# Retention and latent-attention decoder in float32 on one core: x reloaded block by block, three seven-product row pairs in u_1, an ordered first load

## The chip, the cores and the metric

The kernel runs on one core of a Trainium2 chip. The metric is the device time of one execution in microseconds (us); lower is better. In the text PE is the matrix engine (PEld its weight loads), DVE the vector engine, ACT the scalar engine, POOL the GpSimd engine, and SP the engine whose queue issues most transfers. "Granted clock" is the share of PE's full clock that the chip allowed.

## The reference

x is 256 tokens by 2048 features in float32. A retention layer and its MLP are followed by one key and value projection that is shared, an MLA layer and its MLP:

```python
h = rms_norm(x, norm_mix[0])
x = x + retention(h, ret_w_in[0], ret_w_out[0], ret_cos, ret_sin)
x = x + sq_relu_mlp(rms_norm(x, norm_mlp[0]), mlp_w1[0], mlp_w2[0])
k_nope, k_pe, v = mla_shared_kv(rms_norm(x, kv_norm_in), ...)
h = rms_norm(x, norm_mix[1])
x = x + mla_attention(h, ..., k_nope, k_pe, v, mla_cos, mla_sin)
x = x + sq_relu_mlp(rms_norm(x, norm_mlp[1]), mlp_w1[1], mlp_w2[1])

def sq_relu_mlp(h, w1, w2):
    return jnp.square(jax.nn.relu(h @ w1)) @ w2
```

An MLP has 8192 hidden features, so w1 and w2 are 64 MB each, and the two MLPs hold most of the work.

## The kernel before, in words

**Products.** A float32 product is made of three matmuls on operands that are split into a high part and a low part: high x high, high x low, low x high. ACT makes the high part of a weight (CAST ..._wh), DVE subtracts it from the weight to get the low part (TENSOR_TENSOR ..._wl), and both must be there before PE can use them. Weights come in quads: 1 MB, 256 rows by 1024 columns, loaded by one transfer from SP's queue into one of four `raw` buffers. `quad` has two forms. With eight products (24 matmuls of 512 columns) it needs two casts on ACT and two lows on DVE. With seven (a Strassen scheme, 21 matmuls) DVE first adds parts of the weight (`u[0]`, `u[1]`, three instructions) and then there are four casts and four lows.

**Stages.** `gemm_pair` runs eight quads against one pair of sums in PSUM; this is a row pair. An MLP has four groups. Each group has two row pairs of w1 (u_0 and u_1 for the first group, then u_2, u_3 and so on, to u_7) and then two of w2 (d_00, d_01, then d_10 to d_31; the first digit is the group). A layer's number stands behind the letter: u0_7 is u_7 of the first MLP, and u0_73 is quad 3 of it. The views and the orders leave some of the numbers out.

**Hidden blocks.** When a u row pair ends, `pair_out` copies its sums out of PSUM, `summed` joins them, ACT applies relu with the norm's factor (ACTIVATE u_c<-u_c,n_r), copies the result as two 16-bit halves (COPY hid_h<-u_c), four transposing transfers on SP turn them (hid_t), ACT joins the halves (COPY hid_u<-hid_t), squares and casts them, and DVE makes the low part. hid_60 is the first piece of u_6, hid_61 the second; a piece holds two blocks. All this of u_6 runs while PE is in u_7, and that of u_7 while PE is in d_30.

**The residual.** x lies in HBM (`x_home`, tiles xh). d_00 to d_21 add their results there with accumulating transfers from POOL's queue (`to_home`). For the last pair of second products, and likewise for the retention output and the attention output, x must be in SBUF: `x_tiles` allocates four tiles and loads them with eight transfers of 256 KB on POOL's queue (L629, called at L1405 for the MLPs). `bring` is due every two quads.

**The order of the work.** Nothing is issued as it is written. All instructions are recorded in `Plan` with an estimated cost. `forward` is a list scheduler which, on each engine, takes the instruction with the earliest due date among those ready. `latest` runs backward over the result to give better due dates, and both run six rounds (`schedule`); the best is emitted. Each engine then runs its list in order, and waits wherever an operand is not there. All traced instructions therefore have the line L480, that of the emitter. `behind(op, other)` keeps an instruction from being issued ahead of another, and `low_part[0]` is the latest low recorded.

**The start.** `start`, `gemm_two` and `first_inputs` load the first retention weights (rq) and the transposed x (x0t). The first chunk's first half is cut in two, so that the first matmul can start early. DVE casts the positions to float (pos_f), and POOL makes the angles of the rotary tables from them (tab_ang, tab_k, tab_kh); DVE then takes a low part of the table (tab_kl).

Of the kernel before, what the change touches and what calls it, by code (L numbers as in the profile page):

```python
# [120 lines left out]
class Op:  # L121
    __slots__ = ("engine", "method", "args", "kw", "number", "before", "after", "cost", "took", "due", "start", "end",
                 "new", "left", "ready", "made", "held", "moves", "behind", "ahead")


class Plan:
# [19 lines left out]
    def record(self, engine, method, args, kw):  # L146
        op = Op()
        op.engine, op.method, op.args, op.kw = self.ENGINES[engine], (engine, method), args, kw
        op.number, op.before, op.after, op.new = len(self.ops), {}, [], []
        op.made = op.held = None  # L150
        op.behind, op.ahead = set(), []
# [104 lines left out]
    def latest(self):  # L256
# [3 lines left out]
        behind = {op: [] for op in self.ops}  # L260
        limit, free = {}, dict.fromkeys(self.LATENCY, 0.0)
        waiting = {e: [] for e in free}
# [50 lines left out]
    def forward(self):  # L313
# [73 lines left out]
        while True:  # L387
            best = None
            for e in free:
                w, r = waiting[e], ready[e]  # L390
                while w and w[0][0] <= free[e]:
                    _, _, op = heapq.heappop(w)
                    heapq.heappush(r, (op.due, op.number, op))
                at = free[e] if r else w[0][0] if w else None
# [10 lines left out]
            if not ready[e]:  # L405
                while waiting[e] and waiting[e][0][0] <= at:
                    _, _, op = heapq.heappop(waiting[e])
                    heapq.heappush(ready[e], (op.due, op.number, op))
            _, _, op = heapq.heappop(ready[e])
# [138 lines left out]
def yoco(ctx: ExitStack, tc: tile.TileContext, a):  # L548
# [195 lines left out]

    def stream(w, chunk, cols, name, use, done=None, before=None):

        raw = nc.tile(pool, [P, 2048], F32, f"{name}_raw", "raw", 4)
        if before is None:
            nc.sync.dma_start(raw[:, :cols], w[chunk])
        n = cols // 2  # L750
        for half in range(2):
            wh = nc.tile(pool, [P, 1024], F32R, f"{name}_wh{half}", "wh", 5)
            wl = nc.tile(pool, [P, 1024], F32R, f"{name}_wl{half}", "wl", 5)
            cuts = 1
            if before is not None:
                cuts = 1 if half or chunk else 2
                m = n // cuts
                for i in range(cuts):
                    lo = half * n + i * m
                    nc.sync.dma_start(raw[:, lo : lo + m], w[chunk][:, lo : lo + m])  # L760
                    if i == 0:
                        before(half)
            m = n // cuts
            for i in range(cuts):
                lo = half * n + i * m
                low_part[0] = split(wh[:, i * m : (i + 1) * m], wl[:, i * m : (i + 1) * m], raw[:, lo : lo + m])
            use(half, wh, wl)
# [19 lines left out]

    def four_t(acc, act, k0, nk, wh, wl):

        for j in range(4):  # L790
            k = k0 + j
# [24 lines left out]
    def gemm_two(w, act, nk, names, before, done):  # L816
# [3 lines left out]
        for g in range(n):  # L820
            stream(
                w, g, 2048, f"{names[0]}{g}", lambda half, wh, wl: four_t(acc[half], act, g * 4, nk, wh, wl),
                (lambda: done(acc)) if g == n - 1 else None, lambda half: before(g) if half == 0 else None,
            )

# [321 lines left out]
    def first_inputs(c):  # L1147

        t = f2k([2, S], f"x0t_{c}")
        if c:  # L1150
            nc.sync.dma_start(t, a["xt"][:, 2 * c : 2 * c + 2, :])
        else:
            for j in range(2):
                nc.sync.dma_start(t[:, j], a["xt"][:, j, :])
        v = act_tile(f"a0_{c}")
# [656 lines left out]
```

## Time and profile before

| what | value |
|---|---|
| median of 3 runs | 2428.97 us (2428.86 to 2429.07) |
| profiled execution, its own time | 2431.72 us |
| span of the profiled execution | 2429.9 us |
| mean granted clock | 0.996 |
| PE busy | 2405.2 us, 99% |
| DVE busy | 2262.6 us, 93% |
| ACT busy | 1852.3 us, 76% |
| POOL busy | 219.2 us, 9% |
| HBM traffic | 478.09 MB read, 39.85 MB written |

PE is busy nearly all the time, so idle time of another engine matters only where PE ends up waiting for it. "Busy" hides one thing: a matmul at a lower granted clock counts as busy for longer. A row of windows gives, for a stretch A:B, its length, the busy time of PE, PEld, DVE, ACT and POOL (with the number of instructions), the granted clock, the busy share of the DMA engines and GB/s. A row of waits reads: engine, tile, "<-" engine and tile waited for, us in total, times, longest. In a timeline a row holds start, duration, engine, line, operation, out<-in, shapes, and in brackets the idle time ahead of it and what ended that.

### The profile page before, as it was taken

Reading aid. Unit: us, or ns where it says so; the run is one execution under the profiler, and the core shown is the slowest. Engines: PE = TensorE matmul, PEld = TensorE weight load, DVE = VectorE, ACT = ScalarE, POOL = GpSimd, SP = SyncE. Lnnn points to the kernel's source line nnn. Section 1 sums busy time; section 2 is a strip of 40 time slices with the busy share of each in tenths; the row PEclk is TensorE's granted clock in tenths of the full one; section 3 lists DMA queues with packets and bytes.
Section 4 is the critical chain, followed back from the end, with each engine's and each line's share of the span. In section 5 each row is a group of like instructions: output and inputs, shape, how many; then the busy total and the mean of one; then the engine's idle time right before and its main releaser. Section 6 shows DMA issues by size and latency. Waiting matters only on the chain. (4 is left out here: it accounts for less than half of the span.)

```text
span 2429.9 us, 31583 instructions
## 1 busy us (share of the span) xinstructions
PE 2405.2 (99%) x11190; PEld 2013.8 (83%) x11190; DVE 2262.6 (93%) x3002; ACT 1852.3 (76%) x2613; POOL 219.2 (9%) x245
## 2 busy tenths in 40 slices
PE   9999999999999999999999999999999999999999
PEld 7888888888887788888877888998887888888877
DVE  8999999989999999999989998877899999999989
ACT  7666766667787969769769979677879688697795
POOL 3000001011000010010110001110000100100100
PEclk9999999999999999999999999999999999999999
DMA  8566669667585698799897766545767997987974
GB/s 339 191 203 210 204 210 256 201 200 237 200 260 189 220 271 228 242 262 231 239 269 223 217 226 190 169 145 188 220 208 215 257 238 233 258 240 243 265 235 145
DMA packets 197136, 545.18 MB, mean 224 GB/s; under 512 B 115441, under 2 KB 116977, under 8 KB 143729
## 3 DMA queue, kind: packets, MB, share of 16 engines
q1 hardware_dynamic: 174720, 495.84, 63.5%
q0 software_dynamic: 21248, 46.15, 9.9%
q8 instruction: 87, 1.43, 0.2%
q10 hardware_dynamic: 1008, 1.18, 0.2%
q14 instruction: 73, 0.59, 0.1%
HBM read 478.09 MB, written 39.85 MB: 213 GB/s over the span
## 5 line engine op out<-in xcount | busy, mean ns | idle before, releaser
L480 PE MATMUL d_c<-d_wh,hid 128*128 128x512 f32 x1412 | 455.1, 391 | 4.2 <-ACT hid L480 4.2
L480 PE MATMUL u_c<-u_wh,n 128*128 128x512 f32 x1328 | 428.9, 390 | 3.1 <-ACT u_wh L480 3.1
L480 PEld LDWEIGHTS d_c<-d_wh,hid 128*128 128x128 f32 x1412 | 266.5, 189 | 61.4 <-ACT hid L480 5.0
L480 PEld LDWEIGHTS u_c<-u_wh,n 128*128 128x128 f32 x1328 | 249.7, 188 | 55.3 <-ACT u_wh L480 3.8
L480 DVE TENSOR_TENSOR d_wl<-d_raw,d_wh 128x1024 fp32r<-128x1024 f32 (+1 forms) x256 | 279.2, 1108 | 5.4 <-ACT d_wh L480 5.4
L480 ACT CAST u_wh<-u_raw 128x1024 fp32r<-128x1024 f32 (+1 forms) x256 | 235.9, 952 | 62.5 <-PE u_c L480 49.1
L480 DVE TENSOR_TENSOR u_wl<-u_raw,u_wh 128x1024 fp32r<-128x1024 f32 (+1 forms) x256 | 272.6, 1095 | 8.9 <-ACT u_wh L480 8.6
L480 PE MATMUL d_c<-d_wl,hid 128*128 128x512 f32 x706 | 275.8, 391 | 0.1
L480 ACT CAST d_wh<-d_raw 128x1024 fp32r<-128x1024 f32 (+1 forms) x256 | 240.4, 964 | 40.7 <-PE d_c L480 23.2
L480 PE MATMUL u_c<-u_wl,n 128*128 128x512 f32 x664 | 259.4, 391 | 3.1 <-DVE u_wl L480 3.1
L480 PE MATMUL rp_c<-rp_wh,a 128*128 128x512 f32 x640 | 206.6, 390 | 0.0
L480 ACT CAST rp_wh<-rp_raw 128x1024 fp32r<-128x1024 f32 (+1 forms) x128 | 118.4, 944 | 65.6 <-PE rp_c L480 36.7
L480 DVE TENSOR_TENSOR u_wl<-u_u,u_wh 128x1024 fp32r<-128x1024 f32 x120 | 145.3, 1220 | 22.3 <-ACT u_wh L480 21.6
L480 ACT CAST d_wh<-d_u 128x1024 fp32r<-128x1024 f32 x106 | 108.8, 1052 | 69.4 <-DVE d_u L480 59.6
L480 ACT CAST u_wh<-u_u 128x1024 fp32r<-128x1024 f32 x120 | 125.4, 1052 | 43.2 <-PE u_c L480 19.4
L480 PEld LDWEIGHTS d_c<-d_wl,hid 128*128 128x128 f32 x706 | 133.2, 189 | 28.2 <-DVE d_wl L480 0.5
L480 PEld LDWEIGHTS u_c<-u_wl,n 128*128 128x128 f32 x664 | 124.7, 188 | 32.4 <-DVE u_wl L480 6.6
L480 DVE TENSOR_TENSOR rp_wl<-rp_raw,rp_wh 128x1024 fp32r<-128x1024 f32 (+1 forms) x128 | 136.1, 1092 | 8.6 <-ACT rp_wh L480 7.8
L480 PEld LDWEIGHTS rp_c<-rp_wh,a 128*128 128x128 f32 x640 | 120.1, 188 | 26.0 <-DVE rk_u L480 0.9
L480 DVE TENSOR_TENSOR d_wl<-d_u,d_wh 128x1024 fp32r<-128x1024 f32 x106 | 127.6, 1220 | 5.9 <-ACT d_wh L480 5.6
L480 PE MATMUL u_p<-u_wh,n_more 128*128 128x512 f32 x360 | 122.7, 395 | 2.2 <-ACT u_wh L480 2.2
L480 PE MATMUL rp_c<-rp_wl,a 128*128 128x512 f32 x320 | 124.5, 389 | 0.0
(464 smaller groups left out, 5941.4 us busy)
## 6 DMA issues: line engine op xcount, KB each, us to landing
u_raw<-in_mlp_w SPq DMA_DIRECT2D x128, 1024.0 KB, 6.3
d_raw<-in_mlp_w SPq DMA_DIRECT2D x128, 1024.0 KB, 5.3
rp_raw<-in_ret_w_gv SPq DMA_DIRECT2D x64, 1024.0 KB, 5.0
ro_raw<-in_ret_w_out SPq DMA_DIRECT2D x32, 1024.0 KB, 5.1
uq_raw<-in_mla_w_uq SPq DMA_DIRECT2D x24, 768.0 KB, 4.2
rq_raw<-in_ret_w_qk SPq DMA_DIRECT2D x14, 1024.0 KB, 5.7
rk_raw<-in_ret_w_qk SPq DMA_DIRECT2D x14, 1024.0 KB, 5.3
xh<-d_c POOLq DMA_DIRECT2D x48, 256.0 KB, 5.5
```

Of the source, the lines that this page charges most:

```text
L480: op.made = fn(*(real(v) for v in op.args), **{k: real(v) for k, v in op.kw.items()})
```

## The change

It has four parts.

1. `x_tiles`: each of the eight reloads of x is a step of its own, due one quad after the other from the middle of the second quad's turn on, and held behind the latest low part recorded. A layer's reloads thus go one behind each quad of d_30 (the first behind the lows of d_300, the last behind those of d_307), and not in u_7. The same holds for the reloads of the retention output and of wo.
2. In each MLP, u_1 takes seven products in quads 3, 5 and 7 (`SEVEN`) instead of 1, 3, 5 and 7 (`ODD`). Quad 1 is then an eight-product quad.
3. The first transfers get a fixed order (`first`), the first chunk of both halves is cut in two, and the cast of the positions goes from DVE to POOL.
4. `latest` also counts the transfers as the work of one server when it gives due dates. This moves instructions on all engines, throughout the program.

```diff
-            op.due = free[e] = min(limit[op], free[e] - op.cost)
+            op.due = min(limit[op], free[e] - op.cost)
+            if op.moves is not None:
+                server = min(server, op.due + op.cost + op.moves[0]) - op.moves[0]
+                op.due = min(op.due, server - op.cost)
+            free[e] = op.due
...
-                    heapq.heappush(r, (op.due, op.number, op))
+                    heapq.heappush(r, (op.due if op.first is None else op.first - 1e9, op.number, op))
...
             for t in range(NT):
                 x[t][b] = both[:, t].rearrange("p i s -> p (i s)")
-                nc.gpsimd.dma_start(x[t][b], x_home[t][b])
+
+                def load(dst=x[t][b], src=x_home[t][b]):
+                    nc.behind(nc.gpsimd.dma_start(dst, src), low_part[0])
+
+                later(t, load)
 
         for b in range(NB):
-            later(2 * b, lambda b=b: bring(b))
+            later(2 * b + 1, lambda b=b: bring(b))
...
+            raw = nc.tile(pool, [P, 2048], F32, f"{names[0]}{g}_raw", "raw", 4)
...
+            cuts = 1 if g else 2
+            m = 1024 // cuts
+            for i in range(cuts):
+                for half in range(2):
+                    lo = half * 1024 + i * m
+                    ins = nc.sync.dma_start(raw[:, lo : lo + m], w[g][:, lo : lo + m])
+                    if not g:
+                        ins.first = (0, 3, 4, 6)[2 * i + half]
+                    if half == i == 0:
+                        before(g)
...
     def first_tables():
-        nc.vector.tensor_copy(pos_f, pos_i)
+        nc.gpsimd.tensor_copy(pos_f, pos_i)
...
-                seven = (ODD, ODD)[p % 2] if p else LATE
+                seven = (LATE, SEVEN, *(ODD, ODD) * 3)[p]
```

Three places show what this moves. The first is ACT in u0_7, at the casts of quad 3 (u_73_wh) and the first copy of transposed hidden data (hid_60_u). Before:

```order
1205 L480 CAST u_73_wh_11703<-u_73_raw 128x512
1206 L480 COPY hid_61_h_11708<-u_6_c_11592 128x1024
1207 L480 CAST u_73_wh_11719<-u_73_u_11692 128x1024
1208 L480 COPY hid_60_u<-hid_60_t_11648 128x512
1209 L480 COPY hid_61_u<-hid_60_t_11648 128x512
1210 L480 CAST u_73_wh_11743<-u_73_u_11643 128x1024
1211 L480 COPY hid_60_u<-hid_60_t_11659 128x512
```

The same place now:

```order
1201 L484 CAST u_73_wh_11680<-u_73_raw 128x1024
1202 L484 CAST u_73_wh_11690<-u_73_raw 128x512
1203 L484 CAST u_73_wh_11711<-u_73_u_11687 128x1024
1204 L484 CAST u_73_wh_11720<-u_73_u_11655 128x1024
1205 L484 ACTIVATE u_6_c_11595<-u_6_c_11595,n_r 128x512
1206 L484 COPY hid_61_h_11735<-u_6_c_11595 128x1024
1207 L484 COPY hid_60_u<-hid_60_t_11617 128x512
```

All four casts of quad 3 now stand ahead of the first copy of hid_60; before, the last of them stood behind two such copies.

The second place is ACT at the start of d0_00, where the sums of u0_1 (u_1_c) become the halves hid_10_h. Before:

```order
727 L480 CAST d_001_wh_7483<-d_001_raw 128x1024
728 L480 COPY u_1_c_7491<-u_1_c_7128 128x512
729 L480 COPY hid_02_u<-hid_01_t_7374 128x512
730 L480 COPY u_1_p_7504<-u_1_p_7153 128x512
731 L480 COPY hid_02_u<-hid_01_t_7403 128x512
732 L480 CAST d_002_wh_7516<-d_002_raw 128x1024
733 L480 ACTIVATE hid_02_u<-hid_02_u 128x512
734 L480 ACTIVATE u_1_c_7450<-u_1_c_7450,n_r 128x512
735 L480 CAST hid_02_7537<-hid_02_u 128x2x256
736 L480 COPY hid_10_h_7541<-u_1_c_7450 128x1024
```

And now:

```order
730 L484 COPY u_1_c_7468<-u_1_c_7114 128x512
731 L484 COPY u_1_c_7481<-u_1_c_7122 128x512
732 L484 ACTIVATE u_1_c_7468<-u_1_c_7468,n_r 128x512
733 L484 COPY hid_10_h_7492<-u_1_c_7468 128x1024
734 L484 COPY u_1_c_7499<-u_1_c_7128 128x512
735 L484 ACTIVATE u_1_c_7481<-u_1_c_7481,n_r 128x512
736 L484 COPY u_1_c_7515<-u_1_c_7135 128x512
737 L484 COPY hid_10_h_7521<-u_1_c_7481 128x1024
738 L484 CAST d_001_wh_7532<-d_001_raw 128x1024
```

The first copy of u_1's sums stood in row 721 before, and hid_10_h 15 rows behind it; now it is three rows. The cast of piece 10 itself went from row 759 to row 753, that is from 38 rows behind the first copy to 23, because the work on pieces 02 and 03 now lies ahead of the copies.

The third place is SP at the same point, where transposes and weights share a queue. Before:

```order
146 L480 DMA_TRANSPOSE hid_01_t_7403<-hid_01_h_7372 128x4x128
147 L480 DMA d_003_raw<-in_mlp_w_0 128x2048
148 L480 DMA d_004_raw<-in_mlp_w_0 128x2048
149 L480 DMA d_005_raw<-in_mlp_w_0 128x2048
150 L480 DMA_TRANSPOSE hid_10_t_7553<-hid_10_h_7541 128x4x128
151 L480 DMA_TRANSPOSE hid_10_t_7565<-hid_10_h_7541 128x4x128
152 L480 DMA_TRANSPOSE hid_10_t_7553<-hid_10_h_7570 128x4x128
153 L480 DMA_TRANSPOSE hid_10_t_7565<-hid_10_h_7570 128x4x128
154 L480 DMA d_006_raw<-in_mlp_w_0 128x2048
```

And now:

```order
146 L484 DMA d_003_raw<-in_mlp_w_0 128x2048
147 L484 DMA d_004_raw<-in_mlp_w_0 128x2048
148 L484 DMA_TRANSPOSE hid_10_t_7503<-hid_10_h_7492 128x4x128
149 L484 DMA_TRANSPOSE hid_10_t_7519<-hid_10_h_7492 128x4x128
150 L484 DMA_TRANSPOSE hid_10_t_7503<-hid_10_h_7521 128x4x128
151 L484 DMA_TRANSPOSE hid_10_t_7519<-hid_10_h_7521 128x4x128
152 L484 DMA d_005_raw<-in_mlp_w_0 128x2048
```

The four transposes of piece 10 went ahead of the weights of quad 5, which now wait for ACT to have made both halves.

More of the change, by code (lines that the diff above doesn't have):

```diff
@@ L122 @@
     __slots__ = ("engine", "method", "args", "kw", "number", "before", "after", "cost", "took", "due", "start", "end",
-                 "new", "left", "ready", "made", "held", "moves", "behind", "ahead")
+                 "new", "left", "ready", "made", "held", "moves", "behind", "ahead", "first")
 class Plan:
@@ L149, in record @@
         op.number, op.before, op.after, op.new = len(self.ops), {}, [], []
-        op.made = op.held = None
+        op.made = op.held = op.first = None
         op.behind, op.ahead = set(), []
@@ L407, in forward @@
                     _, _, op = heapq.heappop(waiting[e])
-                    heapq.heappush(ready[e], (op.due, op.number, op))
+                    heapq.heappush(ready[e], (op.due if op.first is None else op.first - 1e9, op.number, op))
             _, _, op = heapq.heappop(ready[e])
@@ L753, in stream @@
             wl = nc.tile(pool, [P, 1024], F32R, f"{name}_wl{half}", "wl", 5)
[L754 to L766, printed above, removed]
+            low_part[0] = split(wh[:, :n], wl[:, :n], raw[:, half * n : half * n + n])
             use(half, wh, wl)
@@ L786, in piece, with four_t @@
         stream(w, chunk, 4 * nb, f"{name}{g}", use, done and (lambda: done(acc)))
-    def four_t(acc, act, k0, nk, wh, wl):
-        for j in range(4):
+    def four_t(acc, act, k0, nk, wh, wl, js=range(4)):
+        for j in js:
             k = k0 + j
@@ L820, in gemm_two @@
         for g in range(n):
[L821 to L824, printed above, removed]
+            raw = nc.tile(pool, [P, 2048], F32, f"{names[0]}{g}_raw", "raw", 4)
+            parts = [
+                [nc.tile(pool, [P, 1024], F32R, f"{names[0]}{g}_{i}{half}", i, 5) for i in ("wh", "wl")] for half in range(2)
+            ]
+            cuts = 1 if g else 2
[8 more added lines that the diff above has]
+                        before(g)
+                    wh, wl = parts[half]
+                    low_part[0] = split(wh[:, i * m : (i + 1) * m], wl[:, i * m : (i + 1) * m], raw[:, lo : lo + m])
+            for i in range(cuts):
+                for half in range(2):
+                    four_t(acc[half], act, g * 4, nk, *parts[half], range(i * 4 // cuts, (i + 1) * 4 // cuts))
+            if g == n - 1:
+                queue.append((clock[0] + 0.5, -1, lambda: done(acc)))
+            tick()
     def quad(w, chunk, x, mm, name, split_ends=False):
```

13 lines of the change are left out of this document (7 added, 6 removed).

## The prediction

> **What bounds the kernel now.** I read the page first, then what PE waits for, then the lengths of single stages, and last the timelines of the stages that are too long.
>
> ```profile
> span 2429.9 us, 31583 instructions
> PE 2405.2 (99%) x11190; PEld 2013.8 (83%) x11190; DVE 2262.6 (93%) x3002; ACT 1852.3 (76%) x2613; POOL 219.2 (9%) x245
> ```
>
> PE is the bound over the whole span: 2405.2 of 2429.9 us are matmuls. So a gain can only come from fewer matmuls, from the gaps between them, or from matmuls that run at a lower clock. This is what ended the gaps:
>
> ```profile
> PE d_c L480 <- ACT hid L480: 4.2, 2, 2.4
> PE u_c L480 <- ACT u_wh L480: 3.1, 1, 3.1
> PE u_c L480 <- DVE u_wl L480: 3.1, 5, 0.8
> PE u_p L480 <- ACT u_wh L480: 2.2, 1, 2.2
> PE rq_acc L480 <- DVE a L480: 1.8, 1, 1.8
> ```
>
> Each is short, and few stages hold them. The next rows are row pairs, cut from the first matmul of one to the first matmul of the next: time, PE, PEld, DVE, ACT, POOL, granted clock, DMA share, GB/s. In order they are u0_1, d0_00, u0_5, d0_20, u0_7, d0_30, u1_1, d1_00, u1_7, d1_30.
>
> ```profile
> 754.40:797.19 42.79, 41.50 (x182) 33.48 (x180) 39.82 (x51) 34.80 (x46) 5.10 (x1) 1.00 0.71 219
> 797.19:842.40 45.21, 43.42 (x184) 35.25 (x183) 43.12 (x59) 44.11 (x65) 0.00 (x0) 0.96 0.64 206
> ...
> 1088.53:1129.33 40.80, 40.80 (x182) 33.80 (x180) 40.73 (x50) 39.92 (x56) 0.00 (x0) 1.00 0.93 248
> 1129.33:1170.82 41.49, 41.49 (x184) 34.36 (x183) 40.31 (x53) 38.97 (x55) 0.00 (x0) 1.00 0.85 217
> ...
> 1252.42:1299.35 46.93, 43.72 (x182) 34.40 (x180) 39.86 (x47) 39.52 (x54) 1.08 (x2) 0.96 0.88 254
> 1299.35:1341.66 42.31, 41.98 (x184) 34.20 (x183) 42.01 (x58) 39.64 (x56) 0.00 (x0) 1.00 0.73 221
> 1794.97:1838.27 43.30, 41.90 (x182) 33.40 (x181) 39.70 (x49) 35.07 (x45) 3.88 (x1) 1.00 0.72 199
> 1838.27:1884.22 45.95, 43.56 (x185) 35.34 (x183) 44.17 (x61) 45.05 (x66) 0.00 (x0) 0.96 0.66 210
> ...
> 2293.60:2340.85 47.25, 43.28 (x181) 34.80 (x180) 39.30 (x47) 37.54 (x51) 1.08 (x2) 0.96 0.92 252
> 2340.85:2382.47 41.62, 41.62 (x185) 34.27 (x184) 41.22 (x56) 40.73 (x60) 0.00 (x0) 1.00 0.68 223
> ```
>
> A row pair with 180 weight loads takes 40.80 us when nothing disturbs it (u0_5, PE busy all of it), one with 183 takes 41.49; so a matmul costs (41.49 - 40.80)/3 = 0.23. Against these lengths, u0_7 is 6.13 too long and u1_7 6.45, d0_00 3.72 and d1_00 4.46, u0_1 1.99 and u1_1 2.50, d0_30 0.82 and d1_30 0.13. The granted clock is below 1 in exactly the four worst, and the excess is there larger than the gaps. Three windows of 3.41 us around the wait in d0_00 show why:
>
> ```profile
> 817.95:821.36 3.41, 1.62 (x8) 0.92 (x6) 3.38 (x6) 3.41 (x6) 0.00 (x0) 1.00 0.39 77
> 821.36:824.78 3.42, 3.42 (x10) 2.65 (x9) 3.23 (x5) 3.42 (x6) 0.00 (x0) 0.50 0.60 120
> 824.78:828.19 3.41, 3.41 (x17) 2.79 (x16) 3.41 (x7) 3.41 (x6) 0.00 (x0) 1.00 0.96 360
> ```
>
> After a window in which PE was busy for 1.62 us, the clock is 0.50 for the next one, with 10 matmuls in it where the following holds 17: another 7 x 0.23 = 1.6 us. A wait of about 2 us therefore costs about 3.7, while the waits of 0.8 in u_1 leave the clock at 1.00.
>
> **u_7, the reloads of x.** u0_5 and u0_7 have the same work, except that u0_7 has the reloads beside it. ACT and DVE in u0_7, then POOL, and last how long the hidden transposes take to land in u0_7 and in u0_5:
>
> ```profile
> 1271.54 1.38 ACT L480 COPY hid_u<-hid_t 128x512 uint16<-128x512 uint16 x2 [7.08 <-DMA hid_t<-hid_h]
> 1273.85 1.22 DVE L480 TENSOR_TENSOR u_wl<-u_u,u_wh 128x1024 fp32r<-128x1024 f32 x1 [6.10 <-ACT u_wh L480]
> 1247.67 3.58 POOL L480 DMA_DIRECT2D x_mlp<-xh  x6
> DMA to landing us min/median/max: 2.4/9.1/13.5
> DMA to landing us min/median/max: 3.0/4.6/6.3
> ```
>
> Six reloads go out together, the transposes behind them land in 9.1 instead of 4.6 us, ACT stands 7.08 us at the copy of the first, and behind that copy in ACT's order stands the cast that quad 3 of u0_7 needs; DVE then waits 6.10 for that cast, and PE for both. The change takes both ends off: no reload is issued in u_7, and the cast stands ahead of the copy. With both gone I take u0_5's 40.80 for each u_7: -6.13 - 6.45 = -12.6. If only the order helped, a wait of one to two microseconds could stay; the least gain that I allow is half.
>
> **d_00, the hidden block that comes late.** PE waits 1.8 and 2.4 (the two waits for hid) for hidden piece 10, which ACT makes; ACT is busy 44.11 of 45.21 and 45.05 of 45.95 there, so it is ACT's order that makes the piece late. In the new order the halves of piece 10 are copied out right after u_1's sums, where hidden pieces 02 and 03 were finished first; 38 rows of ACT from the first copy of u_1's sums to the cast of piece 10 become 23. At about 0.7 us a row (44.11/65) that is 10 us earlier, against a lateness of 2.4 at most. The work ahead of it also shrinks: quad 1 of u_1 as eight products needs neither two casts nor the u sums. So the wait goes: -3.72 - 4.46 = -8.2. What is late next is piece 11 or quad 3's lows, which moved ahead as well; I see nothing that must take the wait over.
>
> **u_1, quad 1 as eight products.** DVE's prices in these two stages, by shape:
>
> ```profile
> L480 DVE TENSOR_TENSOR u_wl<-u_u,u_wh 128x1024 fp32r<-128x1024 f32 x8 | 9.7, 1222 | 0.6 <-ACT u_wh L480 0.6
> L480 DVE TENSOR_TENSOR u_u<-u_u,u_raw 128x512 f32<-128x512 f32 x6 | 4.1, 688 | 0.0
> L480 DVE TENSOR_TENSOR u_u<-u_raw 128x1024 f32<-128x1024 f32 x3 | 3.7, 1222 | 0.0
> L480 DVE TENSOR_TENSOR u_wl<-u_raw,u_wh 128x512 fp32r<-128x512 f32 x4 | 2.8, 689 | 1.9 <-ACT u_wh L480 1.9
> ```
>
> A seven-product quad has the sums 1.22 + 2 x 0.69 and the lows 3 x 1.22 + 0.69, together 6.95; an eight-product one has two lows, 2.44. That frees 4.5 us of DVE in a stage where it was busy 39.82 of 42.79, and PE's waits there are five of at most 0.8 for its lows. PE gets three matmuls more, so the stage becomes one of 183: 41.49 instead of 42.79 and 43.30, -1.30 - 1.81 = -3.1, the added 2 x 0.69 already paid. If the waits stay, the added matmuls are a loss of 1.4.
>
> **d_30.** The new due dates bring its transposes forward; d0_30's 0.82 goes if nothing new comes: -0.8.
>
> **New waits.** The eight reloads of a layer now lie in d_30, beside the transposes of the last hidden group, one behind each quad's lows. At the rate of the first row below, 256 KB take 0.65 us of all queues; d0_30 has (1 - 0.73) x 42.31 = 11 us of DMA time spare, and eight loads need 5.2. Behind them on POOL stand only the stores of x, which follow the adds at the end of the stage. But a transpose that meets a load lands 0.65 us later, and in d_20 the new order puts a hidden piece later on DVE. On SP the transposes now stand ahead of several weight transfers, in d_00, d_20 and d_30. For each of the four places (d_20 and d_30, both layers) I know only bounds: nothing, as d0_20 shows now, or a wait like d0_00's with its half clock, 3.7. Nearer to the first, because the two rows of before have 0 and 0.8: I take 0.75 each, together +3. The reloads of the second retention product and of wo go one by one too; there POOL, in order, comes to the roots of retention head 7's norm and of q head 7's norm behind a held reload. PE waits at neither place now; I price them at nothing, and at most one wait of 3.7 each stays for the range.
>
> **The start.** DVE's queue (two rows), PE and POOL, after the row of a stage shortly behind it:
>
> ```profile
> 20.00:40.00 20.00, 20.00 (x106) 17.02 (x105) 20.00 (x32) 14.18 (x26) 8.69 (x10) 1.00 1.03 401
> 6.33 0.17 DVE L480 CAST pos_f<-pos_i 128x2 f32<-128x2 int32 x1 [1.70 <-DMA pos_i<-in_pos]
> 7.70 0.50 PE L480 MATMUL rq_acc<-a,rq_wh 128*128 128x512 f32 x1 [1.81 <-DVE a L480]
> 11.81 1.28 POOL L480 TENSOR_SCALAR tab_kh<-tab_k 128x320 f32<-128x320 f32 x1
> 13.12 0.49 DVE L480 TENSOR_TENSOR tab_kl<-tab_k,tab_kh 128x320 f32<-128x320 f32 x1 [1.18 <-POOL tab_kh L480]
> ```
>
> The cast of the positions moves from DVE to POOL, so the first low no longer waits 1.70 for them, and the first matmul can come up to 1.4 us earlier. But DVE still waits at tab_kl for POOL's chain, with the low of the second quad behind it; PE then only waits there instead of at 7.70. From 20 to 40 us DVE is busy all 20.00, so what DVE did not gain does not reach the end. I take 0, between -1.4 and +1.6 (one more half-clock window).
>
> **The sum.** -12.6 - 8.2 - 3.1 - 0.8 + 3 + 0 = -21.7. The profiled execution took 2431.72, so it would take 2410.0; the median of the runs is 2428.97, 2.75 below the profiled one, and I take the same step from it: **2407.3 us**. Without new waits it is 2404, with the start's best 2403.
>
> **The rivals.** *The stall moves with the reloads.* Eight loads lie beside eight transposes in d_30 as six did in u_7, and ACT's copies of hid_7 stand ahead of d_30's casts; if they cost the same there, 12.6 come back: -21.7 + 12.6 = -9.1, 2420. For it: d_30 has hidden work and SP weights as u_7 had. Against it: its DMA share is 0.73 against 0.88, and each load waits for lows of its own quad, so six cannot go together. The Trainium skill ("DMA: Bandwidth & Descriptors", section "Queues, rings and completion order") says that a DMA engine takes turns between queues packet by packet; by that rule a load delays a transpose wherever they meet, and only the place would change. The trace agrees so far that both queues share one rate. Chance 0.12.
>
> *Slower: weights late behind transposes.* SP issues in order, and a transpose waits for ACT's copy of its half; weight transfers that now stand behind transposes start when ACT has come that far. It decides where a weight lands after the time of its first cast: ACT, DVE and PE then wait in turn as in u_7, about 4 each with the half clock. The new order has such a place in eight stages (the first d of four groups, two layers): 8 x 4 = 32 against 24.7 of gains, +7, 2436. For it: DMA share 0.93 in u0_5 leaves little room to catch up. Against it: up to four weights are loaded ahead, and in u0_5, where weights land in the midst of transposes, PE has no gap. Chance 0.06.
>
> *It does little.* u_7's transposes are slow by themselves, hidden piece 10 stays bound by ACT, and only u_1's 3.1 is won: 2426. Against it stands u0_5 with 4.6 for the same transposes. Chance 0.06.
>
> One rule would price the new waits otherwise: the Trainium skill ("TensorE: Matmul & The Clock Gate", "Part 1: The HAM clock gate") lets the clock fall only after at least one idle window of about 3.4 us. By it the waits of 2 us would cost nothing more than themselves, and the four new waits at most 8 instead of 15. The row at 817.95, busy for 1.62, with 0.50 behind it, speaks against it, and the sum goes by the row.
>
> **How the numbers follow.** The forecast has 0.76, the others 0.12, 0.06 and 0.06. The forecast's own ends are 2403 (no new wait, the start's best) and 2415 (two new waits of 3.7 or half of u_7's gain lost, some 7 more); the first rival must be taken in to hold 8 in 10, with room for it at 2420. The range is 2402 to 2420. A measurement of this kernel tells about 0.2%, 4.9 us: faster has the forecast and the first rival, 0.88; the same is the third, 0.06; slower the second, 0.06.
>
> **What would show it.** Right: u_7 at 40.8 in both layers, no ACT idle of 7 us at a hid_t copy, the clock at 1.00 in u_7 and d_00, u_1 at 41.5, and hid_t landing below 6 us in d_30. Wrong: d_20 or d_30 above 44 with a clock of 0.96 (the first rival), PE waits for ACT's casts that wait for raw weights (the second), or u_7 still above 44 (the third).

## The result, and the profile after

The changed kernel takes 2407.28 us (median of 4 executions, 2405.4 to 2408.16) against 2429.02 (2428.86 to 2430.43): ratio 0.9908, 95% interval 0.9891 to 0.9925. The profiled execution took 2407.68 with a span of 2405.9. A second set of executions gave 2407.6 (0.9908, 0.9893 to 0.9923). The forecast was 2407.3.

The page, and then what PE waits for, in the changed kernel:

```profile
span 2405.9 us, 31599 instructions
PE 2394.7 (100%) x11196; PEld 2010.9 (84%) x11196; DVE 2255.3 (94%) x2992; ACT 1848.6 (77%) x2610; POOL 227.1 (9%) x246
```

```profile
PE rq_acc L484 <- ACT a L484: 1.2, 2, 0.8
...
PE rq_acc L484 <- DVE a L484: 1.1, 2, 0.8
PE n_tp L484 <- ACT n2u L484: 1.0, 1, 1.0
PE u_c L484 <- DVE u_wl L484: 0.8, 1, 0.8
PE u_p L484 <- DVE u_wl L484: 0.5, 1, 0.5
```

The waits for hid and for u_wh have left the list. PE's busy time fell by 10.5 us although six matmuls were added, mostly because the half-clock windows are gone: the execution before had five, one of them in its first 13 us, at about 1.6 us each. The stages of the prediction, in its order (u0_1, d0_00, u0_7, d0_30, then u1_1, d1_00, u1_7, d1_30), cut as before:

```profile
753.62:797.11 43.49, 42.16 (x185) 34.13 (x183) 38.19 (x46) 38.80 (x53) 5.95 (x1) 1.00 0.66 206
797.11:839.02 41.91, 41.79 (x184) 34.28 (x183) 41.26 (x56) 38.98 (x55) 0.00 (x0) 1.00 0.77 222
1248.73:1289.53 40.80, 40.80 (x181) 33.78 (x180) 40.51 (x49) 37.29 (x50) 0.58 (x1) 1.00 0.84 249
1289.53:1331.27 41.74, 41.74 (x184) 34.23 (x183) 40.07 (x53) 41.01 (x59) 3.79 (x7) 1.00 0.83 258
1784.92:1826.40 41.48, 41.48 (x185) 34.35 (x183) 39.32 (x49) 39.73 (x56) 0.00 (x0) 1.00 0.70 220
1826.40:1867.88 41.48, 41.48 (x185) 34.35 (x183) 41.41 (x55) 38.81 (x54) 0.00 (x0) 1.00 0.66 219
2277.32:2318.12 40.80, 40.80 (x181) 33.80 (x180) 40.46 (x50) 38.90 (x53) 0.57 (x1) 1.00 0.84 242
2318.12:2360.07 41.95, 41.80 (x184) 34.24 (x183) 41.18 (x53) 40.16 (x57) 3.80 (x7) 1.00 0.87 268
```

Both u_7 are at 40.80, three of the other four stages with a stall at 41.5 to 41.9, and the clock is 1.00 in all. The hidden transposes land in 4.6 and 5.6 us (medians) in d0_30 and d1_30, below the 6 of the prediction. The first reload of a layer still goes out two to three us before the end of u_7 (POOL's 0.58 and 0.57 in the rows of u_7), the other seven in d_30. One row did not do as forecast: u0_1 is longer than before (43.49, was 42.79).

| term of the sum | forecast | the two profiled executions |
|---|---|---|
| u_7, both layers | -12.6 | -6.13 - 6.45 = -12.6 |
| d_00 | -8.2 | -3.30 - 4.47 = -7.8 |
| u_1 | -3.1 | +0.70 - 1.82 = -1.1 |
| d_30 | -0.8 | -0.57 + 0.33 = -0.2, new waits included |
| new waits in d_20 | part of +3 | 41.49 to 41.56, 41.48 to 41.57: +0.2 |
| the start (first matmul of the first gate and value pair) | 0 | 33.01 to 32.15: -0.9 |
| not in the sum: u0_3, d1_31 | | -0.6, -0.7 |
| span | -21.7 | -24.0 |
| medians | -21.7 | -21.7 |

The medians agree with the sum to 0.1 us only because errors cancel, and so far that is luck. u_1 was forecast too good by 2.0 and d_00 by 0.4; the new waits were too dear by about 2 (0.9 in place of 3), and the start and the two stages that are not in the sum gave another 2.2. The profiles therefore differ by 24.0. The profiled execution of the kernel before took 2.7 more than the median (2431.72; its executions beside the experiments ran from 2426.2 to 2433.2), that of the changed kernel 0.4 more, which brings the medians back to 21.7. The paragraph on the clock takes up the spread.

### The profile page after: what moved, and what is told of

Same layout as the page of the kernel before. It is cut to its first block, busy times and chain, and to the rows that moved or that the text cites. A ratio compares the mean times of both kernels' runs of the same rounds, so it can differ in the third digit from the quotient of the medians.

```text
span 2405.9 us, 31599 instructions
## 1 busy us (share of the span) xinstructions
PE 2394.7 (100%) x11196; PEld 2010.9 (84%) x11196; DVE 2255.3 (94%) x2992; ACT 1848.6 (77%) x2610; POOL 227.1 (9%) x246
## 3 DMA queue, kind: packets, MB, share of 16 engines
q10 hardware_dynamic: 1008, 1.18, 0.1%
## 4 chain that ended last, share of the span: by engine, by line
PE 60%; DVE 4%; ACT 3%; issue 1%; DMA 1%; SPq 0%; ACTq 0%; DVEq 0%
PE d_c L484 19%; PE u_c L484 16%; PE d_p L484 6%; PE u_p L484 5%; PE uq_acc L484 4%; PE ku_acc L484 2%; PE wo_acc L484 2%; PE dqp_c L484 1%; PE dq_acc L484 1%; DVE u_wl L484 1%; PE s L484 1%; DVE d_wl L484 1%; PE kd_acc L484 1%; DVE wop_wl L484 1%; ACT u_wh L484 1%
## 5 line engine op out<-in xcount | busy, mean ns | idle before, releaser
L484 PE MATMUL u_c<-u_wh,n 128*128 128x512 f32 x1352 | 434.8, 389 | 0.0
L484 PE MATMUL u_p<-u_wh,n_more 128*128 128x512 f32 x348 | 116.5, 389 | 0.0
```

The lines of the kernel that those rows point to most:

```text
L484: op.made = fn(*(real(v) for v in op.args), **{k: real(v) for k, v in op.kw.items()})
```

## The experiments

The first four take one part of the change each, or rival it, on the kernel before.

**Reloads alone.** The edit is the x_tiles part of the diff:

```diff
-                nc.gpsimd.dma_start(x[t][b], x_home[t][b])
+
+                def load(dst=x[t][b], src=x_home[t][b]):
+                    nc.behind(nc.gpsimd.dma_start(dst, src), low_part[0])
+
+                later(t, load)
...
-            later(2 * b, lambda b=b: bring(b))
+            later(2 * b + 1, lambda b=b: bring(b))
```

> The kernel before with the first part of the change alone: the reloads of x one by one behind lows. On ACT, SP and PE every instruction stands as before, on DVE all but one add in the retention output. If the reloads are what makes u_7 late, u0_7 falls from 46.93 and u1_7 from 47.25 to 40.8 and the time is about 2429.0 - 12.6 = 2416.4; d_00 keeps its 45.2 and 45.9. If the stall only moves with the reloads, d_30 takes 47 or so in both layers and the time stays within 2427 to 2431. If the order of ACT's copies and casts in u_7 was the cause, u_7 keeps its 47 and the time stays as well.

2417.78 us (2417.13 to 2419.56), ratio 0.9953 (0.9941 to 0.9966). u0_7, d0_30, u1_7, d1_30, and the landing of the hidden transposes in u0_7:

```profile
1254.20:1295.00 40.80, 40.80 (x181) 33.78 (x180) 40.70 (x49) 40.48 (x56) 0.58 (x1) 1.00 0.83 247
1295.00:1336.59 41.59, 41.59 (x184) 34.27 (x183) 40.96 (x57) 38.96 (x54) 3.78 (x7) 1.00 0.86 265
...
2288.12:2328.92 40.80, 40.80 (x181) 33.78 (x180) 40.75 (x49) 38.85 (x52) 0.57 (x1) 1.00 0.85 249
2328.92:2370.42 41.50, 41.50 (x184) 34.35 (x183) 40.21 (x54) 40.06 (x58) 3.79 (x7) 1.00 0.79 258
```

```profile
DMA to landing us min/median/max: 2.5/3.3/5.2
```

ACT, PE and SP run the same instructions in the same order as before, so the reloads were the cause of the stall in the old order, and the stall does not move: d_30, in which seven of the eight loads are issued (the first 2.3 and 2.5 us ahead of it), takes at most 0.1 us more than a clean 41.49. This settles the first rival.

**The order of the copies alone.** One move after the scheduling; `named` gives the recorded instructions of an engine that write a tile of that name:

```diff
+        for layer in range(2):
+            cast = named("ACT", "copy", f"u{layer}_73_wh3")[0]
+            for name in (f"hid{layer}_61_u", f"hid{layer}_60_u"):
+                for o in reversed(named("ACT", "copy", name)):
+                    if order.index(o) < order.index(cast):
+                        order.remove(o)
+                        order.insert(order.index(cast) + 1, o)
```

> The kernel before with one move on ACT in u_7 of each layer: the copies of hid_60 and hid_61 that stood ahead of the last cast of quad 3 go right behind it; the reloads stay in u_7. If the order was a sufficient cause, u_7 falls to 40.8 and the time to 2416.4. If the late transposes are the cause, the same copies now hold up quad 4's casts: PE gets quad 3's rest 3 us earlier and then waits about as long for quad 4, u_7 stays within 45 to 47.5, and the time is 2425 to 2430.

2426.91 (2423.31 to 2431.51), ratio 0.9990 (0.9981 to 0.9999). u0_7 and u1_7:

```profile
1251.08:1297.09 46.01, 43.01 (x181) 34.85 (x180) 40.32 (x48) 40.17 (x56) 1.08 (x2) 0.96 0.94 261
2291.05:2334.38 43.33, 41.69 (x182) 33.64 (x180) 39.53 (x47) 37.78 (x51) 1.08 (x2) 1.00 0.98 274
```

Moved behind one cast, the copies hold up the next quad's casts. The time and u0_7 are as expected; u1_7 is 1.7 us shorter than the range that was expected; in this layer only one copy had stood ahead of the cast. A swap is not enough.

**Due dates alone.**

```diff
-            op.due = free[e] = min(limit[op], free[e] - op.cost)
+            op.due = min(limit[op], free[e] - op.cost)
+            if op.moves is not None:
+                server = min(server, op.due + op.cost + op.moves[0]) - op.moves[0]
+                op.due = min(op.due, server - op.cost)
+            free[e] = op.due
```

> The kernel before with the fourth part alone: due dates that count the transfers as work of one server. If the order is what frees d_00 of its wait, d0_00 and d1_00 fall to 41.5 to 42 and the time to 2429.0 - 8.2 = 2421, with the reloads still in u_7 and u_7 at 46 to 47. If the two casts and five DVE instructions that the third row pair saves in u_1 are what frees d_00, it keeps 45 to 46 here and the time stays within 2427 to 2431.

2425.93 (2423.84 to 2426.98), ratio 0.9983 (0.9974 to 0.9992), less than half of what the first theory gave. d0_00, u0_7, d1_00, u1_7:

```profile
800.39:842.49 42.10, 42.10 (x184) 33.98 (x183) 40.99 (x57) 41.22 (x60) 0.00 (x0) 1.00 0.66 218
1252.00:1301.71 49.71, 44.21 (x181) 35.62 (x180) 39.43 (x47) 39.07 (x53) 1.08 (x2) 0.93 0.88 235
...
1839.85:1884.32 44.47, 42.10 (x185) 34.01 (x183) 42.89 (x60) 44.03 (x65) 0.00 (x0) 1.00 0.68 214
2293.68:2335.28 41.60, 41.42 (x181) 33.52 (x180) 39.90 (x48) 39.43 (x53) 2.14 (x4) 1.00 0.92 282
```

Neither expectation holds as a whole. d0_00 is nearly free, d1_00 still waits 2.4 us for hid; the order of ACT between the first copy of u_1's sums and the cast of piece 10 is still 35 and 39 rows long. With the reloads still in u_7, u0_7 takes 2.8 us more than before and u1_7 only 41.60, where 46 to 47 was expected for both.

**The start alone.** The edit is the third part of the diff (gemm_two, first_inputs, first_tables).

> The kernel before with the third part alone: first transfers in a set order, the first chunk of both halves cut, the cast of the positions on POOL. The first real matmul comes at about 6.1 instead of 7.7, and rp0 starts 0.8 earlier, because DVE waits for POOL's table all the same: 2428.2. If the start were bound by the first matmul alone, it would be 2427.4; if DVE is full up to 75 us and takes everything back, 2429.0. The scheduler moves little behind 100 us, so nothing else should change.

2428.2 (2425.83 to 2431.39), ratio 0.9998 (0.9989 to 1.0006): too small to be told from the times of whole executions. In the profiles the first real matmul comes at 5.86 (was 7.70), and rp0 at 31.04 (was 33.01), in the changed kernel at 32.15. It is worth one to two microseconds in a profile. The expectation had rp0 0.8 earlier, and it came 2.0 earlier, so that the median is the expected one is chance. DVE still waits 1.18 us for POOL's table in this run, but from an earlier point on: its low tab_kl starts at 12.05, where it started at 13.12. In the changed kernel tab_kh ends at 11.21 (13.09 before), and DVE does not wait for it.

**Quad 1 with eight products alone.**

```diff
-                seven = (ODD, ODD)[p % 2] if p else LATE
+                seven = (LATE, SEVEN, *(ODD, ODD) * 3)[p]
```

> The kernel before with the second part alone: quad 1 of u_1 with eight products in both MLPs. By the prediction's step u_1 takes 41.5 in both layers (from 42.79 and 43.30), 2429.0 - 3.1 = 2425.9. If the six added matmuls are not repaid, it is 2429.0 + 1.4 = 2430.4. If the casts and sums that it saves are also what frees d_00, another 8.2 go: 2417.7.

2419.95 (2417.69 to 2421.65), ratio 0.9959 (0.9947 to 0.9972): nearest to the third of the expectations (2417.7). u0_1, d0_00, u1_1, d1_00:

```profile
754.32:797.07 42.75, 42.30 (x184) 34.03 (x183) 38.34 (x48) 38.95 (x54) 5.33 (x1) 1.00 0.66 208
797.07:838.87 41.80, 41.78 (x185) 34.27 (x184) 41.59 (x54) 38.80 (x54) 0.00 (x0) 1.00 0.72 223
...
1791.28:1832.76 41.48, 41.48 (x185) 34.35 (x183) 40.35 (x51) 40.39 (x56) 0.00 (x0) 1.00 0.68 216
1832.76:1874.24 41.48, 41.48 (x185) 34.35 (x183) 41.09 (x54) 37.89 (x53) 0.00 (x0) 1.00 0.70 220
```

The two u_7, with the reloads in them, stay at 46.01 and 47.51. u1_1 comes to the expected 41.5, u0_1 does not; POOL's one instruction in u0_1 is taken up below. So this part frees d_00. With DVE and ACT relieved in u_1, the scheduler finishes pieces 02 and 03 there, and from the first copy of u_1's sums to the cast of piece 10 there are 23 rows in both layers.

**Each part undone in the changed kernel.** Quad 1 of u_1 with seven products again:

> The changed kernel with the second part undone: quad 1 of u_1 takes seven products again. In the changed kernel u0_1 took 43.49 and u1_1 41.48. If the eight-product quad is worth something only where DVE's lows were late, u1_1 comes back to about 43.3 and u0_1 to 42.8, that is +1.8 - 0.7 = +1.1: 2408.4. If it is also what frees d_00, +8 more: 2416.

2414.78 (2413.12 to 2418.38), ratio 0.9941 (0.9929 to 0.9954). u1_1 and d1_00 show the second expectation's case for layer 1, with the 2.4 us wait for hid back in d1_00; d0_00 was 42.45. u0_1, for which 42.8 was expected, took 44.38:

```profile
1786.91:1830.25 43.34, 41.94 (x182) 33.43 (x181) 39.73 (x49) 35.12 (x45) 3.88 (x1) 1.00 0.71 204
1830.25:1874.69 44.44, 42.05 (x184) 33.97 (x183) 42.87 (x60) 44.01 (x65) 0.00 (x0) 1.00 0.67 211
```

The reloads in u_7 again (the deleted lines of x_tiles put back, the new ones taken out):

> The changed kernel with the first part undone: the reloads of x go out together in u_7 again. If the reloads alone decide u_7, it comes back to 46 to 47.5 in both layers and the time to 2407.3 + 12.6 = 2420. If the new order of ACT and SP copes with late transposes, u_7 stays at 41 to 43 and the time below 2412.

2408.34 (2406.96 to 2408.72), ratio 0.9911 (0.9896 to 0.9926): the same as the changed kernel within the intervals, and the second expectation. u0_7 and u1_7, the landing in u0_7, and ACT at the first copy of hid_60:

```profile
1248.79:1289.59 40.80, 40.80 (x181) 33.80 (x180) 40.51 (x49) 37.26 (x50) 3.22 (x6) 1.00 1.08 300
...
2278.10:2318.90 40.80, 40.80 (x182) 33.80 (x180) 40.47 (x48) 38.95 (x54) 2.14 (x4) 1.00 0.93 301
```

```profile
DMA to landing us min/median/max: 7.2/9.1/10.2
```

```profile
1264.65 0.78 ACT L484 COPY hid_u<-hid_t 128x512 uint16<-128x512 uint16 x1
```

The transposes land as late as before (9.1 us), and nobody waits. Three things differ between the kernels with a stall and those without (us from the first matmul of u_7):

| kernel, layer | reloads issued ahead of the transposes | first transpose issued | first copy of hid_60, ACT idle ahead of it | u_7 |
|---|---|---|---|---|
| before, 0 | 6 | 3.9 | 19.12, 7.08 | 46.93 |
| reloads alone, 0 | 0 | 3.9 | 11.93, none | 40.80 |
| copies behind, 0 | 6 | 3.9 | 18.60, 4.42 | 46.01 |
| due dates alone, 0 | 6 | 2.2 | 20.30, 8.02 | 49.71 |
| due dates alone, 1 | 4 | 2.2 | 12.69, 0.41 | 41.60 |
| eight products alone, 0 | 6 | 3.9 | 17.91, 6.83 | 46.01 |
| changed, reloads in u_7, 0 | 2 | 2.2 | 15.86, none | 40.80 |
| changed, reloads in u_7, 1 | 4 | 2.2 | 16.11, none | 40.80 |

In the changed order fewer reloads get ahead of the transposes (the others wait for PE to release their tiles), the transposes go 1.7 us earlier, and the first copy stands 4 us later in ACT's work. The first of the three divides the rows by itself: with six reloads ahead there is a stall, with four or fewer there is none, even where ACT comes to the copy early (due dates alone, layer 1). Layer 1 of the kernels with six reloads fits: 47.25 before, 43.33 and 47.51. The earlier issue does not help by itself: with the due dates alone it is there in layer 0, beside the longest stall. What the later copy would do by itself was not taken apart.

Due dates without the server of the transfers:

> The changed kernel with the fourth part undone: due dates without the server of the transfers. If the order is what frees d_00, d0_00 and d1_00 come back to 45 to 46 and the time to 2407.3 + 8 = 2415. If the other parts do it, the time stays within 2406 to 2410.

2411.4 (2408.58 to 2412.47), ratio 0.9922 (0.9908 to 0.9935). This lies just outside both expected ranges. d_00 stays at 41.48 in both layers, so the order that the due dates give is not needed for it. What the due dates buy lies elsewhere: without them the first matmuls behind x's last norm wait 2.6 us (n_tp for DVE's n; 3.0 longer there), and d1_30 has the wait for hid that I had priced among the new ones:

```profile
2319.67:2364.96 45.29, 43.50 (x185) 35.33 (x183) 42.60 (x56) 39.17 (x55) 3.79 (x7) 0.96 0.78 242
```

Against this stands u0_1, which takes 41.48 here and 43.49 in the changed kernel: the due dates cost 2.0 there.

**Why u0_1 got longer.** POOL's root of the norm and DVE's instructions around it, in the changed kernel (idle time in brackets):

```profile
752.67 6.90 POOL L484 TENSOR_TENSOR n_r<-n_m,neg_half 128x2 f32<-128x2 f32 x1 [28.04 <-DVE n_m L484]
```

```profile
751.82 0.69 DVE L484 TENSOR_TENSOR u_u<-u_p,u_v 128x512 f32<-128x512 f32 x1
752.42 0.16 DVE L484 TENSOR_SCALAR n_m<-n_tot 128x2 f32<-128x2 f32 x1
752.49 0.69 DVE L484 TENSOR_TENSOR u_c<-u_c,u_p 128x512 f32<-128x512 f32 x1
...
758.30 0.69 DVE L484 TENSOR_TENSOR u_v<-u_p,u_v 128x512 f32<-128x512 f32 x1
761.91 1.22 DVE L484 TENSOR_TENSOR u_wl<-u_raw,u_wh 128x1024 fp32r<-128x1024 f32 x1 [2.92 <-ACT u_wh L484]
```

The root works on 128x2 elements and took 6.90 us; the same one in the second MLP (n3_r) took 1.02. It ended 0.58 after the last of a run of eight DVE instructions that, by the kernel, all read two operands from SBUF; beside n3_r, DVE read a sum from PSUM. With the due dates undone the run is of three instructions, DVE then pauses for 0.1 us, and the root takes 2.29. ACT, in order, waited 3.92 for the root, DVE then 2.92 for ACT. The next kernel swaps two DVE instructions, so that the sum from PSUM (u_u) runs beside the root:

```diff
+        norm = named("DVE", "tensor_scalar", "n1_m")[0]
+        order.remove(norm)
+        order.insert(order.index(named("DVE", "tensor_tensor", "u0_0_u")[0]), norm)
```

> The changed kernel with one swap on DVE: the small instruction n1_m, on which POOL's root n1_r waits, goes ahead of the sum u that reads PSUM instead of behind it. In the changed kernel n1_r took 6.90 us on POOL, all of it while DVE ran instructions with two operands in SBUF, and ended 0.57 after DVE fell idle; n3_r in the second MLP, with a sum from PSUM beside it, took 1.02. If POOL is kept out by such instructions, n1_r takes 1 us here, ACT has no 3.9 us wait for it, u0_1 falls from 43.49 to 41.5 and the time to 2407.3 - 2.0 = 2405.3. If the root is slow for another reason (its position in the program, its code), it keeps 5 to 7 and the time stays at 2407.3.

2405.19 (2404.33 to 2408.66), ratio 0.9902 (0.9888 to 0.9915). The root, and u0_1:

```profile
751.86 0.72 POOL L491 TENSOR_TENSOR n_r<-n_m,neg_half 128x2 f32<-128x2 f32 x1 [27.43 <-DVE n_m L491]
```

```profile
753.46:794.94 41.48, 41.48 (x184) 34.36 (x183) 39.16 (x49) 39.76 (x54) 0.00 (x0) 1.00 0.71 225
```

The stage gives the 2.0 us, and d0_00 another 0.4 (41.48). It is the fastest of all the kernels by its median; its interval and the changed kernel's overlap, so the stages, not the medians, show the gain. The same swap on the kernel before, for both norms:

```diff
+        for layer, n in ((0, 1), (1, 3)):
+            for o in (*named("DVE", "reduce_sum", f"n{n}_tot"), *named("DVE", "tensor_scalar", f"n{n}_m")):
+                order.remove(o)
+                order.insert(order.index(named("DVE", "tensor_tensor", f"u{layer}_0_u")[0]), o)
```

> The kernel before with two small DVE instructions moved in each MLP: the total and the mean (n1_tot and n1_m, n3_tot and n3_m) on which POOL's root waits go ahead of the sum u that reads PSUM. The order of all else stays. If POOL is kept out by DVE instructions with two operands in SBUF, n1_r falls from 5.10 and n3_r from 3.88 us to about 1, ACT loses its 3 us wait for them, and the lows of u_1 come in time: u0_1 from 42.79 and u1_1 from 43.30 to 40.8 to 41.3, 2429.4 - 4 = 2425.4. The 26 us of ACT work between the first copy of u_1's sums and the cast of piece 10 are as before, so d_00 should keep its 44 to 46. If DVE's own load makes the lows late, u_1 keeps 42.8 and 43.3 and the time stays within 2427 to 2431.

2425.89 (2424.2 to 2427.88), ratio 0.9985 (0.9976 to 0.9994). The root n1_r, then u0_1 and u1_1:

```profile
756.06 0.72 POOL L488 TENSOR_TENSOR n_r<-n_m,neg_half 128x2 f32<-128x2 f32 x1 [30.11 <-DVE n_m L488]
```

```profile
754.55:795.78 41.23, 41.15 (x181) 33.70 (x180) 39.79 (x51) 34.92 (x46) 0.72 (x1) 1.00 0.81 228
...
1793.50:1834.39 40.89, 40.89 (x181) 33.70 (x180) 39.57 (x49) 35.14 (x45) 0.71 (x1) 1.00 0.74 215
```

With seven-product quad 1 kept and DVE as full as before (39.79 us), PE's waits in u_1 all but vanish. The swap does two things, though: the root is 4.4 us shorter in u0_1 and 3.2 in u1_1, and it also starts more than 5 us earlier. ACT had waited 3.0 for it in each layer, so either would have been enough by these numbers, and this run does not separate them. The swap in the changed kernel does: there the root starts 0.7 earlier against its stage and takes 6.2 less, where ACT had waited 3.92. d_00 kept its wait (44.25 and 45.97), as expected.

**The changed kernel once more**, for its spread:

> The changed kernel itself, beside the kernel before on this chip, for the spread of its executions: about 2407.3, with the stages of its first profile (u0_1 43.5, d0_00 41.9, u_7 40.8 in both layers) to 0.3 us, and no half-clock window behind the first 15 us. If its waits in u0_1 (0.8 and 0.5) can bring a half-clock window, some executions are 1.6 longer.

2407.6 (2406.75 to 2408.69). The stages of the prediction repeat to 0.1 us, except d1_30 (42.29, was 41.95) and, of the others, the second half of the attention output (43.23, was 41.43). There PE waits 1.4 us for DVE's lows (wop_wl), where it waited 0.3; why is open.

**What a wait costs in clock.** Copies of the constants onto themselves delay one cast in each of twelve row pairs:

```diff
...
+                if op.engine == "ACT" and method == "copy":
+                    for _ in range(stalls.get(op.args[0].buf.name, 0)):
+                        self.nc.scalar.copy(self.idle_on.get(), self.idle_on.get())
```

> The changed kernel with 6 to 14 copies of the constants onto themselves on ACT ahead of one cast in each of twelve undisturbed row pairs, 0.48 us a copy. PE needs that cast's low part 2.2 us after it is usually there, so PE idles about 0.7, 1.2, 1.7, 2.1, 2.6, 3.1, 3.6 and 4.5 us (several twice), some 27 us in all. If a window of 3.41 us in which PE is idle for about 1.8 us is followed by one at half the clock, as in the kernel before, the seven waits from 2.1 on cost 1.6 each more: about 2407 + 27 + 11 = 2445. If the clock falls only after a wholly idle window of about 3.4 us (the Trainium skill, TensorE: Matmul & The Clock Gate, Part 1: The HAM clock gate), two at most do: about 2437.

2452.54 in one execution, 7.5 above the first expectation. Eight half-clock windows came where seven had been priced (twice two in a row), and without them the twelve stages are about 32 us longer in place of 27, with a second wait for DVE's low behind most of the first ones. The windows of 3.41 us in which the clock changes lie on one grid through the whole execution. Cut on that grid, pairs of a window with a stall and the one behind it:

```profile
1243.41:1246.83 3.42, 1.60 (x7) 0.75 (x5) 1.28 (x2) 3.39 (x5) 0.00 (x0) 1.00 0.16 29
1246.83:1250.24 3.41, 3.41 (x8) 2.73 (x9) 3.41 (x4) 1.60 (x3) 0.86 (x1) 0.50 0.40 89
...
2083.09:2086.50 3.41, 2.29 (x12) 1.55 (x10) 0.02 (x1) 3.31 (x6) 0.00 (x0) 1.00 0.80 213
2086.50:2089.92 3.42, 2.67 (x10) 1.98 (x11) 3.42 (x4) 2.36 (x3) 0.79 (x1) 1.00 0.21 23
```

In the first pair PE was busy for 1.60 of a window, idle for 1.8, and the next one ran at half the clock. In the second it was busy for 2.29 and 2.67 and there was no fall, though PE idled 1.9 us in all. All six windows with 1.60 us or less (0.32, 0.72, 0.91, 1.20, 1.40, 1.60) were followed by a half-clock one, none of those with 2.25 or more at the full clock. None was wholly idle.

## Why the prediction was right or wrong

**u_7: right in size, and in cause for the old order.** The reloads alone give the -12.6. The prediction said that the change takes both ends off; the experiments add that taking the reloads away is enough, and that the other three parts together are enough too (40.80 with the reloads back in u_7), so in the changed kernel the part on x_tiles no longer earns anything of its own. The cast ahead of the copy is not enough as a swap (46.01). Single parts measured -11.6, -9.4, -3.4 and -1.1 by their medians, together -25.5, the whole -21.7: gains that overlap in u_7 and d_00 don't add.

**d_00: right in size, wrong in which part does it.** The prediction read the shorter stretch of ACT from the order, and named the saved casts second. The stretch of 23 rows comes with the eight-product quad (38 rows before, 35 and 39 with the due dates alone), and the quad alone frees both layers. The due dates alone free d0_00 (42.10) and not d1_00. The gain of about 10 us on the cast was 7.9: against the first matmul of d0_00 it starts at 22.37 before and at 14.44 now.

**u_1: the term that failed.** The step was "That frees 4.5 us of DVE in a stage where it was busy 39.82 of 42.79, and PE's waits there are five of at most 0.8 for its lows". In u_1 there are four such waits, 2.7 us in all; the others of that list lie elsewhere. They are for DVE's lows, but DVE was late because ACT was, and ACT because POOL's root ended late: it took 5.10 and 3.88 us where 0.7 to 1.0 do. In the changed kernel n1_r had no sum from PSUM beside it and took 6.90, so that u0_1 came to +0.70 in place of -1.30. u1_1 came to 41.48 as forecast, but n3_r had a sum from PSUM beside it, so its hit does not confirm the step. Nor did the 4.5 us stay free: DVE's busy time fell by 1.6 in u0_1 (39.82 to 38.19) and by 0.4 in u1_1 (39.70 to 39.32), since the new order put other work there. The row with the price was in the view before: POOL busy 5.10 for one instruction in u0_1, 3.88 in u1_1.

**New waits: mis-sized.** +3 was priced for four places; d_20 measured 0.2 in both together, and d_30 0.2 and 0.5 over 41.49. Their place and price were right in one case: with the old due dates d1_30 is 3.8 above 41.49.

**The start** was taken at 0 because DVE waits for POOL's table and is full from 20 to 40 us. It gave 0.9, and 2.0 by itself: the positions are issued ahead of the frequencies now, POOL's chain ends 1.9 us earlier, and what DVE gains up to 13 us is not lost behind it.

**The rivals.** The stall does not move with the reloads (41.59 and 41.50 in d_30). Weights late behind transposes are not among the waits of the changed kernel: behind its start PE waits 0.5 us or more for the root's sake (u_wl, twice) and once for n2u, which it did before as well (0.8). "It does little" fell with u_7 and d_00.

**The clock.** The price of 1.6 for a half-clock window held (1.5 from 45.95 against 44.47, below). The row at 817.95 already spoke against a rule that needs a whole idle window, and the run with set stalls shows it again: behind 1.60 us busy the clock falls, behind 2.25 it does not. Between these, busy time is no sharp border. Windows with 1.62 to 1.64 fell in three kernels, and this one, in u0_7 of the kernel before with both norms moved, did not:

```profile
1268.59:1272.00 3.41, 1.63 (x8) 1.01 (x6) 0.00 (x0) 2.18 (x3) 0.00 (x0) 1.00 1.05 348
1272.00:1275.42 3.42, 2.37 (x7) 1.23 (x7) 2.38 (x3) 3.42 (x6) 0.00 (x0) 1.00 1.11 383
```

The columns that PE streams in a window divide better. As an estimate from the matmuls of all 14 traces, each spread over its pace of 0.23 us for 512 columns (0.43 at half the clock), the border lies near 3,100 columns, six matmuls of 512. Two rows of the kernel before and of the one with due dates alone, d1_00 in both, show what it does to the spread:

```profile
1858.95:1862.36 3.41, 1.02 (x5) 0.55 (x4) 3.35 (x5) 3.41 (x6) 0.00 (x0) 1.00 0.39 77
```

```profile
1858.65:1862.06 3.41, 2.63 (x11) 1.61 (x9) 3.41 (x4) 3.41 (x6) 0.00 (x0) 1.00 0.37 124
1862.06:1865.48 3.42, 1.83 (x8) 1.42 (x9) 3.30 (x8) 3.42 (x6) 0.00 (x0) 1.00 0.45 90
```

The same wait of 2.4 us falls into one window of the grid in the first and is paid again in clock (d1_00 45.95); in the second it is split over two and costs itself alone (44.47). Where the grid lies differs from one execution to the next. That fits the executions of the kernel before, which spread over 7 us with four such places, while the changed kernel's spread over 3; that the grid makes all of the difference was not shown.

## What to carry to other kernels

A stall that has several conditions can go in more than one way, so price the parts of a change together and expect single gains that don't add. When a small instruction on POOL takes several microseconds, look at which operands DVE reads beside it before blaming the engine that waits last. A wait of about 2 us on PE has two prices, with and without a half-clock window, and the place of the wait on the grid decides; without such waits the executions also spread less here (3 us in place of 7).

## What the runs showed of the hardware

POOL's root of a 128x2 tile ends 0.57 to 0.58 us after DVE's run of instructions with two SBUF operands ends (5.10, 3.88, 6.90, and 5.70 with the due dates alone, 6.31 with the eight products alone), and takes 0.7 to 1.0 where an instruction with a PSUM operand lies beside it. The Trainium skill ("SBUF — State Buffer", section "Who interferes with whom") says that a DVE instruction with two SBUF inputs and a GpSimd instruction that reads SBUF exclude each other for a whole instruction. The traces agree, and show more: POOL was kept out over eight such instructions in a row, not one.

The clock falls for a window of the 3.41 us grid when PE was busy for 1.60 us or less of the window before, and stays at 2.25 or more (run with set stalls); windows with 1.62 to 1.64 did both in other kernels, and by the estimate above some 3,100 matmul columns in a window are the border. The Trainium skill ("TensorE: Matmul & The Clock Gate", "Part 1: The HAM clock gate") puts the fall after at least one idle window; the measurement says that a window about half idle is enough.
